# First k-tile of a mixer and FFN layer: half of its modulation summed on TensorE, larger first transfers, and rk's share of that k-tile moved there

## The chip, the cores and the metric

The kernel runs on one core of a Trainium2 chip. The metric is the device time of one execution in microseconds, the median of three runs. The engines are TensorE (PE; its weight loads are shown apart as PEld), VectorE (DVE), ScalarE (ACT), GpSimd (POOL) and SyncE (SP), which here only issues transfers.

## The reference

One layer over 256 tokens of width 1024, all in float32:

```
mod = silu(c) @ w_ada + b_ada            # six vectors of 1024: sh1, sc1, g1, sh2, sc2, g2
h = x * (1 + sc1) + sh1
y = token_mixer(h, ...)                  # h @ w_in -> mq mk mv rq rk rv rg g_a g_r, then
                                         # attention, retention, gates, two projections, w_out
x = layer_norm(ALPHA * x + g1 * y)
h = x * (1 + sc2) + sh2
y = conv_ffn(h, ...)                     # gate and up (2816 columns), conv of width 3, gelu, down
x = layer_norm(ALPHA * x + g2 * y)
```

w_in has 6656 columns: mq, mk, mv, rq and rk 512 each, then rv, rg, g_a and g_r of 1024. Nothing of h exists until the first two vectors of the modulation do, and these need silu(c) times 1024 x 2048 weights.

## The kernel before

**Precision.** Each float32 product is made of three fp32r products: a weight tile `raw` is split into `whi` (ScalarE copies it, rounding) and `wlo` (VectorE subtracts), the moving or stationary activations into `hh` and `hl`; hi x hi, hi x lo and lo x hi are summed in PSUM. A split of 1024 columns is one ScalarE and one VectorE instruction.

**Phase A (lines 160 to 352)** goes over h's eight k-tiles j of 128 rows. A k-tile's modulation is needed as a column on partitions, so VectorE multiplies the transposed weights of k-tile j (`m<j>`: 128 x 2048, the columns of 1 + sc1 and of sh1) by `srow`, silu(c) spread over all partitions, and sums each row (`ada`, L212; for j = 0 `ada0`, L220 to L228). Then h's k-tile is formed (`h1` parts 1 and 2: `hh`, L253 or L255, and `hl`, L258 and L260), and TensorE multiplies it with k-tile j of three column blocks: a (mq, mk), b (mv, rq) and g (half of g_a's k-tiles 0 to 3), each 1024 columns wide, 12 products of 128 x 512 per block (`x_prod`, L286). Eight PSUM banks `pa` are held through the phase: a and g share banks 0 to 3 (a0's result is copied out at once, L310, and added at the end of the phase, L964), b has banks 4 to 7.

**Transfers.** `UNITS` is the order written by hand in which raw tiles are loaded, four buffers of 1 MB (`RAW_BUFS`) in a ring; `load_A` issues the next one as soon as the program text has passed the last reader of the oldest, and the issue waits on SP's queue for that reader. `m0` is cut in four (`Q4`), its first piece on ScalarE's queue, everything else on SP's; a0 and b0 are one tile, cut in four.

**The start.** Until the modulation's vector c has landed, TensorE runs three matmuls on the identity (`WARM`, L185). Then `rows` (L192) spreads silu(c): eight transposes of a broadcast column (L197) into PSUM banks 6 and 7, `srow_p`. `ada0` has four reductions over 512 columns each, reading `srow_p` from PSUM: the first 512 rows of the weights for both vectors, then the last 512, whence the order of columns in `modT[0]` (L1333); `sums` adds them and the bias. `BUSY` stands for two float32 matmuls on m0's data (L207), whose result is not used. ScalarE copies `srow_p` to `srow` for the later k-tiles (L199).

**Phase B** streams the other weights as units of 1 MB (`weights`, `xstat`, `wstat8`), two halves of 1024 columns each; `prep_halves` splits them (L1206, L1220) up to `LOOKAHEAD` halves ahead. Its first two units are winB's columns of rk: h's eight k-tiles against 512 columns, two products sets (tokens 0 to 127 and 128 to 255) in two banks; at the end `rk_done` (L456) copies the banks into `S["rqk", t]` on ScalarE. Before the first of its products `evac_A` frees phase A's banks, and rope on mq and mk follows on VectorE (L942 to L946).

Of the kernel before, what the change touches and what calls it, by code (L numbers as in the profile page):

```python
# [30 lines left out]
Q4 = (0, 512, 1024, 1536, 2048)  # L31
HALVES = (0, 1024, 2048)
MERGED = 2
BUSY = 2
# [3 lines left out]
UNITS = ("m0", "a0b0", "g0", "m1", "b1g1", "m2", "b2g2", "m3", "b3g3", "a1a2", "m4", "a3", "a4b4", "m5", "a5b5",  # L38
# [18 lines left out]
def _body(nc, a, out, pe, act, dve, sp, cst, wts, big, tmp, ps, dram):  # L57
# [6 lines left out]

    place = {0: ("H", 0), 1: ("H", 1), "3a": ("Ya", 0), "6a": ("Ya", 1), "3b": ("Yb", 0), "6b": ("Yb", 1)}
# [94 lines left out]
    def load_A():  # L160

        if not units:
            return
        u = units.pop(0)
        j = int(u[-1])
        if u[0] != "m" and j and u[:2] != "a1" and u != "a3":
            load_x(j)
        cuts = Q4 if u in ("m0", "a0b0") else HALVES if j < 4 and u[0] in "mb" else (0, 2048)
        t = raw_tile()
        if u in ("g0", "a1a2", "a3"):  # L170
# [5 lines left out]
        for i in range(len(u) // 2):  # L176
            raws[u[2 * i:2 * i + 2]] = t[:, i * 1024:(i + 1) * 1024] if u[0] != "m" else t
# [14 lines left out]
    def rows(dst, cols):  # L192

        ps_ = [bank(6 + c) for c in range(2)]
        for c, p in enumerate(ps_):
            for i in range(4):
                pe.transpose(p[:, i * 128:(i + 1) * 128],  # L197
                             cols[:, c * 4 + i:c * 4 + i + 1].to_broadcast([128, 128]), ident)
        return ps_, lambda c: act.activation(dst[:, c * 512:(c + 1) * 512], ps_[c], AF.Copy)  # L199
# [3 lines left out]
    srow_p, srow_copy = rows(srow, sc)  # L203

    for i in range(BUSY):
        raw = raws["m0"]
        pe.matmul(bank(5), raw[:, i * 128:i * 128 + 128], raw[:, :512], start=True, stop=True)  # L207
# [7 lines left out]
    sums = cst.tile([128, 2, 3], F32, name="sums")  # L215
    dve.tensor_scalar(sums[:, :, 2], bcol[:, 0:2, 0], 0.0, None, op0=OP.add)

    def ada0(raw):

        junk = tmp.tile([128, 1024], mybir.dt.bfloat16, name="junk", bufs=1)  # L220
        for q in range(2):
            for i in range(2):
                w = raw[:, (2 * q + i) * 512:(2 * q + i + 1) * 512]
                dve.tensor_tensor_reduce(out=junk[:, :512], in0=srow_p[q], in1=w, scale=1.0, scalar=0.0,
                                         op0=OP.mult, op1=OP.add, accum_out=sums[:, i, q:q + 1])
            if q == 0:
                srow_copy(0)
        dve.tensor_reduce(mod[:, 0:2, 0], sums, mybir.AxisListType.X, OP.add)  # L228
# [35 lines left out]
    def halve(name, w=1024, between=None):  # L264

        raw = raws.pop(name)
        hi, lo = whl[name] = new_hl()
        for c in range(0, 1024, w):
            o = slice(c, c + w)
            act.activation(hi[:, o], raw[:, o], AF.Copy)  # L270
# [4 lines left out]
    def x_prod(name, ks, first=False, last=False, w=1024):  # L275


        j, b0, ws = int(name[1]), dict(a=0, b=4, g=0)[name[0]], whl[name]
        x = [hh, hh, hl]
        what = dict(zip((2, 1, 3), (((0, 0), (1, 1)), ((2, 0),), ((0, 0), (1, 1), (2, 0)))))[ks]  # L280
        turns = [(xi, k, c, t) for c0 in range(0, 1024, w) for xi, k in what for c in range(c0, c0 + w, 512)
                 for t in range(2)]
        if ks == 3:
            turns.sort(key=lambda e: e[2:])
        for xi, k, c, t in turns:
            pe.matmul(pa[b0 + c // 512 * 2 + t], x[xi][:, j, t * 128:(t + 1) * 128], ws[k][:, c:c + 512],  # L286
                      start=first and (xi, k) == (0, 0), stop=last and xi == 2)
# [7 lines left out]

    h1(0, 0)
    h1(0, 1)
    halve("a0", 512)
    srow_copy(1)
    h1(0, 2)  # L300
# [10 lines left out]
    g_prod(0, 2)  # L311
    g_prod(0, 1)
# [42 lines left out]
    main = []  # L355
    steps = []

    def weights(src, mm0, mm1):

        n = 2 * len(main)  # L360
        main.append(src)
        for i, mm in enumerate((mm0, mm1)):
            steps.append(((n + i,), (n + i,), lambda ts, mm=mm: mm(*ts[0])))
# [10 lines left out]
    def xstat(name, u0, xh, xl, nk, banks_of, done):  # L374
        for u in range(nk // 4):
            def mk(half, u=u):
                def mm(hi, lo):
                    bk = banks_of()
                    for t in range(2):
                        for kk in range(2):  # L380
                            k = u * 4 + half * 2 + kk
                            mm3(bk[t], xh(k)[:, t * 128:(t + 1) * 128], xl(k)[:, t * 128:(t + 1) * 128],
                                hi[:, kk * 512:(kk + 1) * 512], lo[:, kk * 512:(kk + 1) * 512],
                                k == 0, k == nk - 1)
                    if k == nk - 1:
                        done(bk)
                return mm
            weights(a[name][u0 + u], mk(0), mk(1))
# [62 lines left out]
    S = {}  # L451
    ghh, ghl = (lambda k: hh[:, k]), (lambda k: hl[:, k])

    def rk_done(bk):
        for t in range(2):
            act.activation(S["rqk", t][:, 512:1024], bk[t], AF.Copy)  # L456

    xstat("winB", 0, ghh, ghl, 8, lazy(two_banks), rk_done)
# [498 lines left out]
    def evac_A():  # L957
        v = slot(4, [128, 2, 512])
        for t in range(2):
            S["rqk", t] = slot(f"R{t}", [128, 1024])  # L960
        for t in range(2):
            for c in range(2):
                o = qk[t][:, c * 512:c * 512 + 512]
                dve.tensor_tensor(o, pa[2 * c + t], o, OP.add)  # L964
# [204 lines left out]
    for sec, at in ((2, (6, 7, 9, 10)), (3, (11, 12, 13, 14)), (4, (16, 18, 19, 20)), (5, (38, 41, 44, 47))):  # L1169
        for u in range(4):  # L1170
            done = (lambda sec=sec: rows_done(sec)) if sec > 3 else (lambda: None)
            extra.setdefault(at[u], []).append((a["ada2"][sec - 2, u], ada_unit(sec, u, done)))
    stream = []
    for i, src in enumerate(main):
        stream.append((src, None))
# [4 lines left out]
    def load_next():  # L1180
        if stream:
            src, fn = stream.pop(0)
            loaded.append((load_raw(src), fn))

    def prep_halves():
# [4 lines left out]
        def raw_halves():  # L1190
            while loaded:
                raw, fn = loaded.pop(0)
                for half in range(2):
                    if fn:
                        chain.append((raw, half, fn))
                    else:
                        yield raw[:, half * 1024:(half + 1) * 1024], half
# [3 lines left out]
        def first():  # L1201
            src, half = next(it, (None, None))
# [3 lines left out]
            act.activation(hi, src, AF.Copy)  # L1206
            return src, half, hi

        ahead = None
        while True:  # L1210
# [7 lines left out]
            src, half, hi = cur  # L1218
            lo = wts.tile([128, 1024], F32R, tag="wlo", name="wlo", bufs=HL_BUFS)
            dve.tensor_tensor(lo, src, f(hi), OP.subtract)  # L1220
# [152 lines left out]
```

## Time and profile before

| | |
|---|---|
| median of 3 runs | 427.49 us (427.38 to 427.71) |
| the profiled execution | 428.27 us |
| its span, first to last instruction | 426.5 us |
| TensorE busy | 416.9 us |
| VectorE busy | 368.1 us |
| ScalarE busy | 244.8 us |
| bytes read from HBM | 104.15 MB, 247 GB/s over the span |

Times in the views are in microseconds from the start of the span. In a timeline each line is: start, duration, engine, line of the code, operation, output <- inputs, shape, count, and in brackets the idle time of the engine before it with what ended it. Lines of the same kind are merged, so the duration of an "x4" runs from the first start to the last end. The chain of work that ended last is followed back from the last instruction and lists start, duration and what was running. Window lines give each engine's busy time, the granted clock, the DMA engines' busy share and GB/s. Transfer lines give the size and the time from issue to landing.

### The profile page before, as it was taken

To read this page: it belongs to the slowest core of one execution; us is meant where nothing else is said; L and a number is where in the kernel's file an instruction comes from. 1 tells how busy PE (TensorE), PEld (TensorE's weight loads), DVE (VectorE), ACT (ScalarE), POOL (GpSimd) and SP (SyncE) were. 2 spreads that over 40 slices of the span, in tenths; PEclk is the share of its full clock that TensorE was granted. 3 is DMA by queue.
4 is the path that set the end of the run, shared out by engine and by line. 5 is a ranking of instruction groups with operands and counts; after the bars stand their busy time and mean duration, and the time that the engine had idled before them with its cause. 6 is when DMAs were issued, how large, how long until landed. Compare 5 with 4: busy or idle time off the path is not lost.

```text
span 426.5 us, 5818 instructions
## 1 busy us (share of the span) xinstructions
PE 416.9 (98%) x2130; PEld 348.9 (82%) x2130; DVE 368.1 (86%) x608; ACT 244.8 (57%) x389; POOL 7.2 (2%) x18
## 2 busy tenths in 40 slices
PE   8999999999999999999999999999999999999992
PEld 4787888877878888888889899888888888888882
DVE  5888999979997999898778887999999888789576
ACT  4667558779764488534353885654545545455400
POOL 0000000100000000001000000100000000000000
PEclk9999999999999999999999999999999999999998
DMA  8999988869468868789552085985876776440001
GB/s 271 407 410 366 408 289 354 311 273 303 171 238 330 288 250 314 285 341 378 211 197 100 1 290 204 350 295 190 310 254 232 281 287 232 191 191 2 1 26 74
DMA packets 19694, 105.60 MB, mean 248 GB/s; under 512 B 2641, under 2 KB 4561, under 8 KB 8913
## 3 DMA queue, kind: packets, MB, share of 16 engines
q1 hardware_dynamic: 18144, 99.97, 62.5%
q0 software_dynamic: 1376, 4.99, 3.5%
q8 instruction: 17, 0.28, 0.3%
q10 hardware_dynamic: 144, 0.26, 0.2%
q14 instruction: 13, 0.10, 0.1%
HBM read 104.15 MB, written 1.06 MB: 247 GB/s over the span
## 4 chain that ended last, share of the span: by engine, by line
PE 96%; DMA 2%; DVE 1%; issue 0%; ACT 0%; POOL 0%; DVEq 0%; POOLq 0%
PE P L111 17%; PE P L113 17%; PE P L112 17%; PE P L120 15%; PE P L286 11%; PE P L122 8%; DMA raw<-in_strm 2%; PE P L665 1%; PE P L668 1%; PE P L667 1%; PE P L952 1%; PE P L1004 1%; PE P L1023 1%; PE P L1047 1%; PE P L207 1%; PE P L185 1%
## 5 line engine op out<-in xcount | busy, mean ns | idle before, releaser
L1220 DVE TENSOR_TENSOR wlo<-raw,whi 128x1024 fp32r<-128x1024 f32 x118 | 141.9, 1218 | 13.7 <-ACT whi L1206 13.6
L1206 ACT ACTIVATE whi<-raw 128x1024 fp32r<-128x1024 f32 x118 | 122.8, 1056 | 44.1 <-PE P L113 19.7
L111 PE MATMUL P<-whi,AH 128*128 128x512 f32 (+1 forms) x168 | 65.9, 392 | 0.0
L113 PE MATMUL P<-whi,AH 128*128 128x512 f32 (+1 forms) x168 | 64.0, 381 | 0.0
L112 PE MATMUL P<-wlo,AH 128*128 128x512 f32 (+1 forms) x168 | 63.8, 380 | 0.0
L212 DVE CUSTOM_DVE_ANT_0 junk<-raw,srow 128x1024 bf16<-128x1024 f32 x46 | 56.0, 1218 | 0.2
L286 PE MATMUL P<-whi,AH 128*128 128x512 f32 x160 | 42.5, 392 | 0.4 <-ACT AH L255 0.3
L120 PE MATMUL P<-AYa,whi 128*128 128x512 f32 x144 | 39.2, 394 | 0.0
L120 PE MATMUL P<-AYb,whi 128*128 128x512 f32 x144 | 38.6, 390 | 0.0
L111 PEld LDWEIGHTS P<-whi,AH 128*128 128x128 f32 x168 | 31.6, 188 | 6.7 <-issue 1.3
L113 PEld LDWEIGHTS P<-whi,AH 128*128 128x128 f32 x168 | 31.6, 188 | 6.2
L286 PEld LDWEIGHTS P<-whi,AH 128*128 128x128 f32 x160 | 29.8, 188 | 8.4 <-ACT AH L255 1.2
L112 PEld LDWEIGHTS P<-wlo,AH 128*128 128x128 f32 x168 | 31.7, 189 | 5.5
L436 ACT ACTIVATE A<-P 128x256 f32<-128x256 f32 x36 | 13.7, 381 | 34.1 <-PE P L122 32.2
L120 PEld LDWEIGHTS P<-AYb,whi 128*128 128x128 f32 x144 | 27.0, 188 | 6.0
L270 ACT ACTIVATE whi<-raw 128x1024 fp32r<-128x1024 f32 (+1 forms) x26 | 21.8, 857 | 16.8 <-DMA raw<-in_strm 15.0
L273 DVE TENSOR_TENSOR wlo<-raw,whi 128x1024 fp32r<-128x1024 f32 (+1 forms) x26 | 24.7, 977 | 5.8 <-ACT whi L270 5.5
L120 PEld LDWEIGHTS P<-AYa,whi 128*128 128x128 f32 x144 | 25.1, 190 | 3.6
L122 PEld LDWEIGHTS P<-AYa,wlo 128*128 128x128 f32 x144 | 22.0, 189 | 2.8
L286 PE MATMUL P<-wlo,AH 128*128 128x512 f32 x80 | 23.5, 391 | 0.1
L122 PE MATMUL P<-AYb,wlo 128*128 128x256 f32 x144 | 23.1, 283 | 0.0
L122 PE MATMUL P<-AYa,wlo 128*128 128x256 f32 x144 | 22.9, 282 | 0.0
(269 smaller groups left out, 712.3 us busy)
## 6 DMA issues: line engine op xcount, KB each, us to landing
raw<-in_ada SPq DMA_DIRECT2D x16, 1024.0 KB, 5.6
raw<-in_wup SPq DMA_DIRECT2D x11, 1024.0 KB, 5.8
raw<-in_wgate SPq DMA_DIRECT2D x11, 1024.0 KB, 5.7
raw<-in_wdown SPq DMA_DIRECT2D x11, 1024.0 KB, 4.9
raw<-in_winB SPq DMA_DIRECT2D x10, 1024.0 KB, 6.5
raw<-in_strm SPq DMA_DIRECT2D x8, 1024.0 KB, 7.0
raw<-in_strm SPq DMA_DIRECT2D x12, 512.0 KB, 7.6
raw<-in_winGr SPq DMA_DIRECT2D x4, 1024.0 KB, 6.2
```

The lines of the kernel that those rows point to most:

```text
L111: pe.matmul(o, lh, rh, start=start, stop=False)
L112: pe.matmul(o, lh, rl, start=False, stop=False)
L113: pe.matmul(o, ll, rh, start=False, stop=stop)
L120: pe.matmul(o, wh[:, k * 128:(k + 1) * 128], x2[k], start=k == 0, stop=False)
L122: pe.matmul(o[:, :256], wl[:, k * 128:(k + 1) * 128], x2[k][:, 0], start=False, stop=k == n - 1)
L212: dve.tensor_tensor_reduce(out=junk[:, rows], in0=raw[:, rows], in1=srow[:, rows], scale=1.0, scalar=0.0, op0=OP.mult, op1=OP.add, accum_o ...
L270: act.activation(hi[:, o], raw[:, o], AF.Copy)
L273: dve.tensor_tensor(lo[:, o], raw[:, o], f(hi[:, o]), OP.subtract)
L286: pe.matmul(pa[b0 + c // 512 * 2 + t], x[xi][:, j, t * 128:(t + 1) * 128], ws[k][:, c:c + 512], start=first and (xi, k) == (0, 0), stop=la ...
L436: act.activation(t, p[:, 256:], AF.Copy)
L1206: act.activation(hi, src, AF.Copy)
L1220: dve.tensor_tensor(lo, src, f(hi), OP.subtract)
```

## The change

- `m0` is one transfer of 1 MB on ScalarE's queue. a0 and b0's tile is cut in two instead of four. g0's tile becomes `r0g0`: k-tile 0 of rk's 512 columns, then g0.
- Only the first four transposes are made ahead of the sum (`spread(0)`). `ada0` sums the first 512 rows of the weights on VectorE (two reductions) and the last 512 on TensorE: eight float32 matmuls with a 128 x 128 block of weights as stationary operand and one column of silu(c) as moving operand, into two columns of bank 5. A matmul of 128 x 128 on m0's data follows, whose result is not used. VectorE adds the bias and then bank 5. `BUSY` and `sums` are gone.
- The other four transposes (`spread(1)`) come after a0's first four products; both copies to `srow` come after a0.
- `x_prod("r0", ...)` makes rk's six products of k-tile 0 in banks 0 and 1, after b0's; ScalarE copies them into `S["rqk", t]`, whose slots are opened earlier.
- Phase B's first unit leaves out k-tile 0: its transfer, its split and its six products. `rk_done` adds the banks on VectorE to what lies in `S["rqk", t]`.

The diff, without the parts that only pass the new column offset on:

```diff
-Q4 = (0, 512, 1024, 1536, 2048)
-BUSY = 2
-UNITS = ("m0", "a0b0", "g0", "m1", "b1g1", ...
+UNITS = ("m0", "a0b0", "r0g0", "m1", "b1g1", ...
...
-        cuts = Q4 if u in ("m0", "a0b0") else HALVES if j < 4 and u[0] in "mb" else (0, 2048)
+        cuts = HALVES if u == "a0b0" or j < 4 and u[0] in "mb" else (0, 2048)
...
-    def rows(dst, cols):
-        ps_ = [bank(6 + c) for c in range(2)]
-        for c, p in enumerate(ps_):
-            for i in range(4):
-                pe.transpose(p[:, i * 128:(i + 1) * 128],
-                             cols[:, c * 4 + i:c * 4 + i + 1].to_broadcast([128, 128]), ident)
-        return ps_, lambda c: act.activation(dst[:, c * 512:(c + 1) * 512], ps_[c], AF.Copy)
+    def spread(c):
+        p = bank(6 + c)
+        for i in range(4):
+            pe.transpose(p[:, i * 128:(i + 1) * 128],
+                         sc[:, c * 4 + i:c * 4 + i + 1].to_broadcast([128, 128]), ident)
+        return p
...
-    srow_p, srow_copy = rows(srow, sc)
-    for i in range(BUSY):
-        raw = raws["m0"]
-        pe.matmul(bank(5), raw[:, i * 128:i * 128 + 128], raw[:, :512], start=True, stop=True)
+    srow_p = [spread(0)]
...
     def ada0(raw):
         junk = tmp.tile([128, 1024], mybir.dt.bfloat16, name="junk", bufs=1)
-        for q in range(2):
-            for i in range(2):
-                w = raw[:, (2 * q + i) * 512:(2 * q + i + 1) * 512]
-                dve.tensor_tensor_reduce(out=junk[:, :512], in0=srow_p[q], in1=w, scale=1.0, scalar=0.0,
-                                         op0=OP.mult, op1=OP.add, accum_out=sums[:, i, q:q + 1])
-            if q == 0:
-                srow_copy(0)
-        dve.tensor_reduce(mod[:, 0:2, 0], sums, mybir.AxisListType.X, OP.add)
+        acc = bank(5)
+        for i in range(2):
+            for k in range(4):
+                w = raw[:, 1024 + (2 * k + i) * 128:1024 + (2 * k + i + 1) * 128]
+                pe.matmul(acc[:, i:i + 1], w, sc[:, 4 + k:5 + k], start=k == 0, stop=k == 3)
+        pe.matmul(bank(4)[:, :128], raw[:, :128], raw[:, :128], start=True, stop=True)
+        for i in range(2):
+            dve.tensor_tensor_reduce(out=junk[:, :512], in0=srow_p[0], in1=raw[:, i * 512:(i + 1) * 512], scale=1.0,
+                                     scalar=0.0, op0=OP.mult, op1=OP.add, accum_out=mod[:, i, 0:1])
+        m = mod[:, 0:2, 0]
+        dve.tensor_tensor(m, m, bcol[:, 0:2, 0], OP.add)
+        dve.tensor_tensor(m, acc[:, :2], m, OP.add)
...
     halve("a0", 512)
-    srow_copy(1)
     h1(0, 2)
+    a0 = whl["a0"]
+    for c in (0, 512):
+        for t in range(2):
+            pe.matmul(pa[c // 512 * 2 + t], hh[:, 0, t * 128:(t + 1) * 128], a0[0][:, c:c + 512], start=True, stop=False)
+    srow_p.append(spread(1))
+    for xi, k in ((hh, 1), (hl, 0)):
+        for c in (0, 512):
+            for t in range(2):
+                pe.matmul(pa[c // 512 * 2 + t], xi[:, 0, t * 128:(t + 1) * 128], a0[k][:, c:c + 512], start=False,
+                          stop=xi is hl)
+    srow_copy(0)
+    srow_copy(1)
     halve("b0", 512)
     load_A()
+    halve("r0")
     halve("g0")
     load_A()
-    x_prod("a0", 2, True, False, 512)
-    x_prod("a0", 1, False, True, 512)
-    x_prod("b0", 2, True, False, 512)
+    x_prod("b0", 2, True, False)
     x_prod("b0", 1)
     for i in range(4):
         act.activation(qk[i % 2][:, i // 2 * 512:i // 2 * 512 + 512], pa[i], AF.Copy)
-    g_prod(0, 2)
-    g_prod(0, 1)
+    x_prod("r0", 3, True, True, cs=(0,))
+    for t in range(2):
+        act.activation(S["rqk", t][:, 512:], pa[t], AF.Copy)
+    x_prod("g0", 3, True, cs=(512, 0))
...
     def rk_done(bk):
         for t in range(2):
-            act.activation(S["rqk", t][:, 512:1024], bk[t], AF.Copy)
+            o = S["rqk", t][:, 512:1024]
+            dve.tensor_tensor(o, bk[t], o, OP.add)
-    xstat("winB", 0, ghh, ghl, 8, lazy(two_banks), rk_done)
+    xstat("winB", 0, ghh, ghl, 8, lazy(two_banks), rk_done, 1)
```

More of the change, by code (lines that the diff above doesn't have):

```diff
@@ L175, in load_A @@
         load_cuts(t, src, cuts, (lambda: load_x(0)) if u == "a0b0" else None, act if u == "m0" else sp)
-        for i in range(len(u) // 2):
-            raws[u[2 * i:2 * i + 2]] = t[:, i * 1024:(i + 1) * 1024] if u[0] != "m" else t
+        c = 0
+        for n in (u[i:i + 2] for i in range(0, len(u), 2)):
+            w = dict(m=2048, r=512).get(n[0], 1024)
+            raws[n] = t[:, c:c + w]
+            c += w
     for i in range(RAW_BUFS):
@@ L267, in halve @@
         hi, lo = whl[name] = new_hl()
-        for c in range(0, 1024, w):
-            o = slice(c, c + w)
+        n = raw.shape[-1]
+        for c in range(0, n, min(w, n)):
+            o = slice(c, c + min(w, n))
             act.activation(hi[:, o], raw[:, o], AF.Copy)
@@ L273, in halve, with x_prod @@
             dve.tensor_tensor(lo[:, o], raw[:, o], f(hi[:, o]), OP.subtract)
-    def x_prod(name, ks, first=False, last=False, w=1024):
-        j, b0, ws = int(name[1]), dict(a=0, b=4, g=0)[name[0]], whl[name]
+    def x_prod(name, ks, first=False, last=False, w=1024, cs=(0, 512)):
+        j, b0, ws = int(name[1]), dict(a=0, b=4, g=0, r=0)[name[0]], whl[name]
         x = [hh, hh, hl]
         what = dict(zip((2, 1, 3), (((0, 0), (1, 1)), ((2, 0),), ((0, 0), (1, 1), (2, 0)))))[ks]
-        turns = [(xi, k, c, t) for c0 in range(0, 1024, w) for xi, k in what for c in range(c0, c0 + w, 512)
-                 for t in range(2)]
         if ks == 3:
-            turns.sort(key=lambda e: e[2:])
+            turns = [(xi, k, c, t) for c in cs for t in range(2) for xi, k in what]
+        else:
+            blocks = [cs] if w == 1024 else [(c,) for c in cs]
+            turns = [(xi, k, c, t) for b in blocks for xi, k in what for c in b for t in range(2)]
         for xi, k, c, t in turns:
@@ L293, in _body @@
     ga = slot(12, [128, 4, 512])
+    for t in range(2):
+        S["rqk", t] = slot(f"R{t}", [128, 1024])
     h1(0, 0)
@@ L310, in _body @@
         act.activation(qk[i % 2][:, i // 2 * 512:i // 2 * 512 + 512], pa[i], AF.Copy)
-    g_prod(0, 2)
-    g_prod(0, 1)
+    x_prod("r0", 3, True, True, cs=(0,))
+    for t in range(2):
+        act.activation(S["rqk", t][:, 512:], pa[t], AF.Copy)
+    x_prod("g0", 3, True, cs=(512, 0))
     WB = (512, 1024, 1024, 512)
@@ L387, in mk @@
                 return mm
[L388 removed]
+            weights(a[name][u0 + u], mk(0), mk(1), 512 * k0 if u == 0 else 0)
     bank_i = [0]
@@ L1191, in raw_halves @@
             while loaded:
-                raw, fn = loaded.pop(0)
+                raw, fn, c0 = loaded.pop(0)
                 for half in range(2):
@@ L1196, in raw_halves @@
                     else:
-                        yield raw[:, half * 1024:(half + 1) * 1024], half
+                        yield raw[:, half * 1024:(half + 1) * 1024], half, slice(0 if half else c0, 1024)
         it = raw_halves()
         def first():
-            src, half = next(it, (None, None))
+            src, half, o = next(it, (None,) * 3)
             if src is None:
```

46 lines of the change are left out of this document (25 added, 21 removed).

## The prediction

> **What bounds the kernel now.** I read the head of the page, the chain of work that ended last, the timeline of the first 18 us, and then the DMA and window views of the same stretch.
>
> ```profile
> span 426.5 us, 5818 instructions
> PE 416.9 (98%) x2130; PEld 348.9 (82%) x2130; DVE 368.1 (86%) x608; ACT 244.8 (57%) x389; POOL 7.2 (2%) x18
> PE 96%; DMA 2%; DVE 1%; issue 0%; ACT 0%; POOL 0%; DVEq 0%; POOLq 0%
> ```
>
> TensorE is busy for 98% of the span and carries 96% of the chain. So only two things can move the time: when TensorE gets its first real product, and how long it stands or runs slowly after that.
>
> ```profile
> 3.93 1.95 PE P L197 x8
> 5.87 1.72 PE P L207 x2
> 7.64 1.14 PE P L207 x2
> 8.79 7.46 DMA raw<-in_strm
> 17.25 0.59 ACT AH L255
> 17.89 16.79 PE P L286 x72
> 34.68 30.24 PE P L286 x132
> ```
>
> The chain has one interruption in 65 us: the transfer issued at 8.79 (b1g1's first half), then ScalarE's modulated x of the second k-tile (L255), then products without a break. 132 products in 30.24 us are 0.229 us each; that is the pace used below.
>
> ```profile
> 5.06 0.69 DVE L224 CUSTOM_DVE_ANT_0 junk<-P,raw 128x512 bf16<-128x512 f32 x1 [0.92 <-PE P L197]
> 7.36 0.69 DVE L224 CUSTOM_DVE_ANT_0 junk<-P,raw 128x512 bf16<-128x512 f32 x1
> 8.09 0.16 DVE L228 TENSOR_REDUCE mod<-sums 128x2 f32<-128x6 f32 x1
> 8.29 0.60 DVE L253 TENSOR_SCALAR AH<-AYa,mod 128x128 fp32r<-128x128 f32 x2
> 8.78 0.70 PE L286 MATMUL P<-whi,AH 128*128 128x512 f32 x2
> 9.54 0.73 PE L286 MATMUL P<-wlo,AH 128*128 128x512 f32 x2
> 16.28 1.06 ACT L270 ACTIVATE whi<-raw 128x1024 fp32r<-128x1024 f32 x1 [1.24 <-DMA raw<-in_strm]
> 17.89 1.20 PE L286 MATMUL P<-whi,AH 128*128 128x512 f32 x4 [0.34 <-ACT AH L255]
> ```
>
> Before the first product, VectorE decides: four reductions from 5.06 to 8.05, their sum at 8.09, x modulated at 8.29, first product 8.78. The start of the reductions is held by the transposes (L197), not by a transfer. From 8.78 to 17.89 stand 36 products (a0, b0, g0), 36 x 0.229 = 8.24, so 0.87 us of the 9.11 is lost: about 0.4 in a0, where the third product starts at 9.54 instead of 9.24, and about 0.5 ahead of 17.89.
>
> **The change, part by part.**
>
> *m0 as one transfer.* It is needed whole now, because TensorE's half lies behind VectorE's.
>
> ```profile
> 1.25 1.88 SPq L98 DMA_DIRECT2D raw<-in_strm  x4
> raw<-in_strm ACTq DMA_DIRECT2D x1, 256.0 KB, 2.9
> raw<-in_strm SPq DMA_DIRECT2D x1, 256.0 KB, 4.2
> 4.00:8.00 4.00, 3.94 (x11) 2.30 (x12) 2.88 (x9) 1.15 (x2) 0.00 (x0) 1.00 1.00 321
> 12.00:16.00 4.00, 4.00 (x19) 3.32 (x18) 2.94 (x5) 3.00 (x5) 0.00 (x0) 1.00 1.03 413
> ```
>
> The piece on ScalarE's queue landed 2.9 us after its issue at 0.80, at 3.7; m0's last piece, the third of the four SP issues (1.25 + 2 x 0.47 = 2.2), landed 4.2 later, at 6.4. With 2 KB rows the engines moved 321 GB/s (4 to 8 us), with longer rows 413 (12 to 16). The remaining 0.79 MB at 413 GB/s take 1.9 us: 5.6 if m0 has the engines to itself. It doesn't: a0b0's first half stands on SP's queue from 1.25. If that half's 0.52 MB all go between, 6.9. I take 6.1, near the old 6.4, with 5.6 and 6.9 as ends. The Trainium skill, "DMA: Bandwidth & Descriptors", section "Queues, rings and completion order", says that a DMA engine serves its queues in turn, packet by packet; by that m0 gives up a part of the bandwidth and 5.6 is not reached. The traces here can't show it for these two queues, as their large transfers don't overlap before the change.
>
> *The sum on TensorE.* Four reductions become two (2 x 0.77 = 1.5, done by 7.6 and so covered); TensorE gets eight matmuls of one column.
>
> ```profile
> 1.42 0.29 PEld L185 LDWEIGHTS P<-ident 128*128 128x128 f32 x1 [1.42 <-POOL ident L141]
> 1.42 0.50 PEld L185 LDWEIGHTS P<-ident 128*128 128x128 f32 x2 [1.42 <-POOL ident L141]
> 3.90 1.97 PE L197 MATMUL P<-ident,sc 128*128 128x128 f32 x8
> 75.64 1.03 PE L952 MATMUL P<-ident,A2a 128*128 128x128 f32 x8
> 5.67 1.06 PE L207 MATMUL P<-raw 128*128 128x512 f32 x1
> 8.17 0.59 PE L207 MATMUL P<-raw 128*128 128x512 f32 x1
> ```
>
> An f32 matmul is two passes, each with its weight load (L185: three matmuls, six loads), so 16 passes. A one-column pass is nowhere in this trace. Eight 128-column passes take 1.97 us early (0.25 each) and 1.03 at 75 us (0.13 each); a second load ended 0.21 after the first. Bounds: 16 x 0.13 = 2.1 and 16 x 0.25 = 3.9. I take 0.14 and a tail of 0.2, 2.5 us, near the lower end, because 127 of the 128 streamed columns fall away. The final add then stands where the reduce stood, and from there to the first product went 8.78 - 8.09 = 0.69. First product: 6.1 + 2.5 + 0.06 + 0.69 = 9.35, so 0.57 later than before. Ends: 5.6 + 2.1 + 0.75 = 8.45 and 6.9 + 3.9 + 0.75 = 11.55. While TensorE sums, nothing else in its queue could run: the filler matmul and a0's products stand behind.
>
> *BUSY's two matmuls go.* They lay inside the wait, so they cost nothing; but the rows of L207 show what they covered. The same shape takes 1.06 at 5.67 and 0.59 at 8.17, and the transposes above 0.25 and 0.13: TensorE ran at half rate until after 6.5 us and at full rate from about 7.64, although the windows print a granted clock of 1.00 there. Half rate ended after some 3.7 us of unbroken work (3.93 to 7.64 in the chain); the stretch before, with pauses, had not ended it. After the change TensorE has four transposes (to about 4.8), then nothing until m0 lands, then one-column passes. I charge 0.3 us for about 0.6 us of a0 at half rate; ends 0 and 1.85 (3.7 us of products at half rate lose half).
>
> *The other four transposes* move in behind a0's first four products: 4 x 0.13 = 0.52 at full rate, in a place where about 0.4 was lost anyway. *r0:* six products (6 x 0.229 = 1.37) go from the first winB half, where TensorE never stood, to the first k-tile. From the first product to the second k-tile's first: 42 x 0.229 + 0.52 = 10.14, so 19.49. Before, with the same six products added, it was 17.89 + 1.37 = 19.26. Net **+0.23**.
>
> *What must be ready at 19.49.*
>
> ```profile
> 13.01 0.58 ACT L310 ACTIVATE A2a<-P 128x512 f32<-128x512 f32 x1
> 23.44 0.76 PEld L286 LDWEIGHTS P<-whi,AH 128*128 128x128 f32 x4 [0.24 <-ACT AH L255]
> 28.94 0.30 PEld L286 LDWEIGHTS P<-whi,AH 128*128 128x128 f32 x2 [0.18 <-ACT AH L255]
> ```
>
> b1's transfer: its slot is m0's, free when the filler matmul ends (about 9.3; before, 8.79), and it queues behind transfers already issued, so the later issue costs nothing. The first 2.2 MB move at 413 instead of 321 GB/s (1.5 us sooner), r0's 0.26 MB cost 0.6: it lands about 0.9 earlier than 16.26. The tighter path is ScalarE's: two copies of r0's banks now stand ahead of b1's whi. r0's products end at 9.35 + 0.52 + 30 x 0.229 + 0.4 = 17.1; copies about 0.6 after the second bank, whi 1.06, x 0.58: 19.4, just under 19.49. Taken as 0; if it slips, 0.6. The two short waits at 23.44 and 28.94 (0.24 and 0.18, of which TensorE's stream shows about half) go, as TensorE now arrives later: **-0.2**. SP gets fewer issues (m0 1 for 4, a0b0 2 for 4), POOL none.
>
> *winB's end of it.*
>
> ```profile
> 62.43 1.28 DVE L964 TENSOR_TENSOR A2a<-P,A2a 128x512 f32<-128x512 f32 x2
> 68.55 2.35 DVE L1220 TENSOR_TENSOR wlo<-raw,whi 128x1024 fp32r<-128x1024 f32 x2
> 70.42 0.39 PE L112 MATMUL P<-wlo,AH 128*128 128x512 f32 x1
> 76.77 1.07 ACT L456 ACTIVATE AR<-P 128x512 f32<-128x512 f32 x2
> ```
>
> The third half's wlo ends about 69.75 and is used at 70.42: 0.67 of slack. VectorE's way there starts with a7's banks (62.43), and TensorE now has 1.37 us less to do between a7 and that half. VectorE took a7's banks without an idle gap (the row at 62.43 has no bracket), so it, not TensorE, was late there before, and a part is absorbed; taken as 0, ends 0 and 0.7. The first half's split is 512 columns shorter on both engines. rk's bank is added on VectorE (2 x 0.68) instead of copied on ScalarE (2 x 0.55), at a place where later halves are far ahead: 0.
>
> **Sum:** +0.23 - 0.2 + 0.3 = +0.33 us. The profiled execution took 428.27 (span 426.5 and 1.77 around it), 0.78 over the median; the difference is carried to the median: 427.49 + 0.33 = 427.8.
>
> **The rivals.**
> *Half rate stays (slower).* The pause from 4.8 to 6.1 and the one-column passes don't count as the work that ended half rate before, and a0 and b0 begin at half rate for another 3.7 us: +1.85 instead of +0.3, 429.4. For it: L185's stretch with pauses did not bring full rate. Against: the passes and the filler keep the queue busy for 3 us. It decides once more than 1.4 us of half-rate loss come together, given the other terms.
> The Trainium skill, "TensorE: Matmul & The Clock Gate", section "What's actually happening", says the clock starts at half and is released after a window of about 3.4 us of sustained work that runs free of the program; by that figure an unlucky window would cost 1.7, an estimate, and the time be about 429.2. The L207 rows agree with a halved start.
> *m0 early (faster).* m0 alone at 5.6 and TensorE's passes no longer than VectorE's 1.5: first product 5.6 + 1.6 + 0.75 = 7.95, 1.4 sooner than in the sum, no half-rate products: 427.49 + 0.33 - 0.3 - 1.4 = 426.1; with the passes at 0.13, 426.6. For it: larger rows move 413. Against: a0b0 shares the engines and the early passes ran 0.25.
> *The gap returns.* ScalarE's r0 copies delay b1's whi: the moved products then fill nothing, +0.6: 428.4.
>
> **How the numbers follow.** What this measurement can tell from no change is about 0.2%, 0.85 us: 426.6 to 428.3. The sum's case 0.31 (own range 427.0 to 428.4); half rate stays 0.31; m0 early 0.28; the gap returns 0.10, split between same and slower. So faster 0.28, same 0.36, slower 0.36. Range 426.2 to 429.9: the early case without its last tenth, and the half-rate case with half a microsecond of late summing.
>
> **What would show it.** In the timeline after: the one-column matmuls start between 5.6 and 6.9; the first L286-type product near 9.35; the product spacing there 0.23 (0.45 if half rate stays); no idle ahead of b1's first product near 19.5; winB's first half six products shorter and no wait on wlo near 70. It is wrong if the first product comes before 8.5 or after 10.2, or if the spacing stays at 0.45 for over 1.5 us.

## The result: 1.15% slower, and the profile after

| | median | range | ratio to before, 95% interval |
|---|---|---|---|
| before | 427.49 us | 427.29 to 427.71 | |
| after | 432.47 us | 432.04 to 432.78 | 1.0115 (1.0102 to 1.0128) |

Each row has five executions. The change costs 4.98 us; the prediction was 427.8 with a range of 426.2 to 429.9. The profiled execution of after took 432.78 us. The head of its page and its line of the chain's shares:

```profile
span 431.1 us, 5836 instructions
PE 420.3 (98%) x2144; PEld 353.3 (82%) x2144; DVE 367.6 (85%) x607; ACT 243.4 (56%) x390; POOL 7.2 (2%) x18
PE 88%; DVE 6%; DMA 3%; issue 1%; ACT 1%; DVEq 0%; SPq 0%; ACTq 0%
```

TensorE is still busy for 98%. Its 14 extra instructions are worth little, and yet it is busy for 3.4 us more: the same work got slower. Where, the chain that ended last shows in order of time (start, duration, what ran):

```profile
1.24 4.79 DMA raw<-in_strm
6.17 3.54 PE P L222 x16
9.71 0.64 PE P L223 x2
10.44 2.05 PE P L308 x4
12.48 0.85 PE P L198 x4
13.34 3.03 PE P L313 x8
16.36 23.15 PE P L289 x102
39.52 26.83 PE P L289 x117
```

m0's transfer, the sixteen one-column passes (L222), the filler, a0's products (L308, L313), then products without a break. In before this chain had VectorE's reductions covered by the filler and its first product at 8.78. TensorE's timeline of the same stretch (PEld's rows are left out):

```profile
4.68 1.11 PE L198 MATMUL P<-ident,sc 128*128 128x128 f32 x4 [0.76 <-DVE sc L192]
6.17 3.54 PE L222 MATMUL P<-sc,raw 128*128 128x1 f32 x16 [0.37 <-DMA raw<-in_strm]
9.57 0.78 PE L223 MATMUL P<-raw 128*128 128x128 f32 x2
10.44 2.05 PE L308 MATMUL P<-whi,AH 128*128 128x512 f32 x4
12.28 1.06 PE L198 MATMUL P<-ident,sc 128*128 128x128 f32 x4
12.99 2.06 PE L313 MATMUL P<-wlo,AH 128*128 128x512 f32 x4
14.84 1.52 PE L313 MATMUL P<-whi,AH 128*128 128x512 f32 x4
16.20 1.09 PE L289 MATMUL P<-whi,AH 128*128 128x512 f32 x4
```

The first product comes at 10.44, 1.66 later than in the profile of before. And four products of one shape take 2.05 at 10.44 and 2.06 at 12.99, but 1.09 at 16.20: TensorE is at half rate until nearly 16 us. The gap of 0.34 ahead of k-tile 2 is gone (TensorE's rows have no bracket from 6.17 to 24 us), and no wait stands at winB's third half; what was lost by then stayed lost. VectorE and ScalarE at the same place:

```profile
7.30 0.16 DVE L228 TENSOR_TENSOR mod<-mod,first 128x2 f32<-128x2 f32 x1
9.75 0.16 DVE L229 TENSOR_TENSOR mod<-P,mod 128x2 f32<-128x2 f32 x1 [2.28 <-PE P L222]
4.22 0.21 ACT L191 ACTIVATE sc<-first 128x8 f32<-128x8 f32 x1 [1.49 <-DMA first<-in_first]
```

VectorE's half of the sum is ready at 7.46 and waits 2.28 us for TensorE's. ScalarE gets the vector c at 4.22; in before it did at 3.44.

### The profile page after: what moved, and what is told of

It is laid out like the page before. It is cut to its first block, busy times and chain, and to the rows that moved or that the text cites. A ratio compares the mean times of both kernels' runs of the same rounds, so it can differ in the third digit from the quotient of the medians.

```text
span 431.1 us, 5836 instructions
## 1 busy us (share of the span) xinstructions
PE 420.3 (98%) x2144; PEld 353.3 (82%) x2144; DVE 367.6 (85%) x607; ACT 243.4 (56%) x390; POOL 7.2 (2%) x18
## 4 chain that ended last, share of the span: by engine, by line
PE 88%; DVE 6%; DMA 3%; issue 1%; ACT 1%; DVEq 0%; SPq 0%; ACTq 0%
PE P L119 15%; PE P L110 14%; PE P L112 14%; PE P L111 14%; PE P L289 12%; PE P L121 8%; DVE wlo L1240 3%; DMA raw<-in_winB 2%; DMA raw<-in_strm 1%; PE P L687 1%; PE P L690 1%; PE P L689 1%; PE P L222 1%; PE P L1043 1%; PE P L313 1%
## 5 line engine op out<-in xcount | busy, mean ns | idle before, releaser
L1240 DVE TENSOR_TENSOR wlo<-raw,whi 128x1024 fp32r<-128x1024 f32 (+1 forms) x118 | 141.4, 1213 | 13.6 <-ACT whi L1226 13.3
L1226 ACT ACTIVATE whi<-raw 128x1024 fp32r<-128x1024 f32 (+1 forms) x118 | 122.2, 1053 | 44.0 <-PE P L112 19.7
L110 PE MATMUL P<-whi,AH 128*128 128x512 f32 (+1 forms) x166 | 65.2, 393 | 0.0
L112 PE MATMUL P<-whi,AH 128*128 128x512 f32 (+1 forms) x166 | 63.2, 380 | 0.0
L289 PE MATMUL P<-whi,AH 128*128 128x512 f32 x156 | 41.3, 390 | 0.0
L110 PEld LDWEIGHTS P<-whi,AH 128*128 128x128 f32 x166 | 31.2, 188 | 6.6 <-issue 1.3
L112 PEld LDWEIGHTS P<-whi,AH 128*128 128x128 f32 x166 | 31.2, 188 | 6.2
L289 PEld LDWEIGHTS P<-whi,AH 128*128 128x128 f32 x156 | 29.3, 188 | 6.5 <-ACT A L348 0.4
L275 DVE TENSOR_TENSOR wlo<-raw,whi 128x1024 fp32r<-128x1024 f32 (+1 forms) x27 | 25.2, 966 | 7.8 <-ACT whi L272 7.6
L272 ACT ACTIVATE whi<-raw 128x1024 fp32r<-128x1024 f32 (+1 forms) x27 | 21.8, 844 | 12.5 <-DMA raw<-in_strm 12.5
```

The lines of the kernel that those rows point to most:

```text
L110: pe.matmul(o, lh, rh, start=start, stop=False)
L112: pe.matmul(o, ll, rh, start=False, stop=stop)
L1226: act.activation(hi[:, o], src[:, o], AF.Copy)
L1240: dve.tensor_tensor(lo[:, o], src[:, o], f(hi[:, o]), OP.subtract)
```

## The experiments

Theory: the loss is TensorE's rate. It runs at half rate until it has worked densely for a while, and one-column passes are not such work, while the matmuls of `BUSY`, which they replaced, were. Rival: the order of things at the start (m0 as one transfer, c late, the sum waiting) delays the first product, and the rest is the moved rk. Each ratio below is against executions of before that were taken together with the run; their medians are 427.51 to 427.75 us.

### One part at a time

**Before without BUSY.**

```diff
-BUSY = 2
+BUSY = 0
```

> The kernel before with BUSY = 0, nothing else changed. Half-rate theory: the first product stays near 8.7 us, since VectorE's four reductions set it, but TensorE stands from 5.9 to 8.7 and a0 and part of b0 then run at half rate (0.43 us between products instead of 0.23) for 3.5 to 5.5 us; 1.5 to 2.5 us slower, 429.0 to 430.0. Rival (the two BUSY matmuls are only filler, and full rate comes on its own or is not needed because a0 waits for wlo anyway): within 0.4 us of 427.5.

Measured 429.08 us, ratio 1.0037 (1.0023 to 1.005). TensorE's timeline:

```profile
8.82 1.19 PE L286 MATMUL P<-whi,AH 128*128 128x512 f32 x2 [2.91 <-DVE AH L253]
12.37 2.07 PE L286 MATMUL P<-whi,AH 128*128 128x512 f32 x6
14.28 0.62 PE L286 MATMUL P<-wlo,AH 128*128 128x512 f32 x2
```

The first product is where it was (8.82), yet 1.6 us are lost: two products take 1.19 here against 0.70 in before, and 0.62 only from 14.28. The two filler matmuls were no decoration: they brought the full rate before the first product.

**After with the start of before** (m0 and a0b0 in four, `rows`, four reductions, BUSY, a0's products in their old order; r0 and phase B as in after):

```diff
-    srow_p = [spread(0)]
+    srow_p, srow_copy = rows(srow, sc)
+    for i in range(BUSY):
+        pe.matmul(bank(5), raw[:, i * 128:i * 128 + 128], raw[:, :512], start=True, stop=True)
...
-                pe.matmul(acc[:, i:i + 1], w, sc[:, 4 + k:5 + k], start=k == 0, stop=k == 3)
+                dve.tensor_tensor_reduce(out=junk[:, :512], in0=srow_p[q], in1=w, ..., accum_out=sums[:, i, q:q + 1])
```

> The kernel after with the start of the kernel before: m0 and a0b0 in four pieces, all eight transposes first, four reductions on VectorE, BUSY. Left of the change: rk's six products of k-tile 0, their tile r0g0, the shorter first winB unit, the add on VectorE. If the loss is all in the start (half rate and late sum): 0.3 to 0.9 us faster than before, 426.6 to 427.2, since the six products fill the 0.5 us ahead of the second k-tile. If moving rk costs (ScalarE's copies ahead of b1, VectorE's add, wlo late for the third half): 0.5 to 1.5 us slower, 428.0 to 429.0.

427.72 us, 1.0012 (0.9997 to 1.0026): the same as before. Moving rk's columns neither costs nor brings what a measurement can tell; the expected gain of the closed gap did not come (see the repeated before below).

**Before with the sum on TensorE alone** (transfers of before, rk in phase B, no BUSY):

```diff
-    srow_p, srow_copy = rows(srow, sc)
+    srow_p = [spread(0)]
-    for i in range(BUSY):
...
+                pe.matmul(acc[:, i:i + 1], w, sc[:, 4 + k:5 + k], start=k == 0, stop=k == 3)
```

> The kernel before with the sum half on TensorE and the transposes split as in the change, BUSY gone, but m0 and a0b0 still in four pieces and rk not moved. Late-sum and half-rate theory together: c lands at 3.4 as before, m0's last piece at 6.4, sixteen passes of 0.22 us, first product near 10.7, half rate until 14 to 16 us; 3.5 to 5 us slower, 431 to 432.5. If the larger transfers are what makes the change slow: under 1 us slower, 427.5 to 428.5.

430.69 us, 1.0079 (1.0062 to 1.0095): the largest part, though less than the 431 to 432.5 that was expected. The first product stands at 9.98 instead of near 10.7, and half rate ends at about 12.6 instead of 14 to 16.

**Before with the larger transfers alone** (and four reductions on VectorE, BUSY, rk as in before):

```diff
-        cuts = Q4 if u in ("m0", "a0b0") else HALVES if j < 4 and u[0] in "mb" else (0, 2048)
+        cuts = HALVES if u == "a0b0" or j < 4 and u[0] in "mb" else (0, 2048)
```

> The kernel before with m0 as one transfer on ScalarE's queue and a0b0 in two, nothing else. c lands 0.8 us later, as in the changed kernel; the four reductions start when m0 is whole, near 6.1, and end near 9.1, first product near 9.8; BUSY's matmuls run from 6.1 to 9 and keep TensorE busy, so no product at half rate. If the start alone counts: about 1 us later, of which 0.5 is given back at the second k-tile: 427.9 to 428.6. If larger rows speed the first k-tiles up: 426.5 to 427.3.

428.33 us, 1.0021 (1.0012 to 1.003). c lands 0.57 later, and VectorE's reductions and the first product (9.34) move with it; the rate is full. Against their befores (427.51) the three parts give 3.18 + 0.82 + 0.21 = 4.21 of 4.98. They don't add up in full, and one difference is seen: half rate, which ends at about 12.6 with the sum alone, lasts to nearly 16 in after.

### What counts as work for the rate

**Passes 128 columns wide**, all else as in after:

```diff
-                pe.matmul(acc[:, i:i + 1], w, sc[:, 4 + k:5 + k], start=k == 0, stop=k == 3)
+                pe.matmul(acc[:, i * 128:(i + 1) * 128], w, sc[:, 4 + k:5 + k].to_broadcast([128, 128]),
+                          start=k == 0, stop=k == 3)
```

> After, with each of the sixteen weight passes 128 columns wide instead of one (the same weights, the silu column repeated 128 times; VectorE adds columns 0 and 128 of the sums). The arithmetic is the same. Theory (one-column passes do not count as work for the granted clock, 128-column passes do): a pass takes about as long as before at half rate (0.21 to 0.22 us against 0.22), the first product stays at 10.2 to 10.6, but the rate doubles earlier than the 15.76 of after, at 9.5 to 13, so that 1 to 2.5 us of the half-rate stretch go: 430.0 to 431.5. Rival A (the width does not matter, the rate is released a fixed time after products begin): product spacing 0.43 until about 15.8, 432.2 to 432.8. Rival B (a wide pass costs by its columns, 0.4 us): the passes end at 12.5, the first product at about 13, 433 to 435.

429.45 us, 1.0048 (1.0033 to 1.0063): **3.0 us of the 4.98 come back when each pass streams 128 times as many columns.** Its executions took 429.05 to 430.42 us, those of after 432.04 to 432.78. TensorE's timeline:

```profile
6.08 2.98 PE L222 MATMUL P<-sc,raw 128*128 128x128 f32 x16 [0.37 <-DMA raw<-in_strm]
9.79 1.15 PE L309 MATMUL P<-whi,AH 128*128 128x512 f32 x4 [0.51 <-DVE AH L255]
13.05 1.07 PE L290 MATMUL P<-whi,AH 128*128 128x512 f32 x4
```

The passes begin at the same place (6.08 against 6.17) and take no longer (2.98 against 3.54), and the first four products take 1.15, not 2.05. From first product to the first one of b0 are 3.26 us, in after 16.20 - 10.44 = 5.76: 2.5 us of half rate. The time that came back is more than the 1 to 2.5 us of the theory, as the rate doubled ahead of the first product.

**Passes 32 columns wide.**

```diff
+                pe.matmul(acc[:, i * 32:(i + 1) * 32], w, sc[:, 4 + k:5 + k].to_broadcast([128, 32]), ...
```

> After, with the passes 32 columns wide (1 column: 432.47; 128 columns: 429.45). Theory (what counts for the granted clock is the time in which columns stream, and 32 columns fill a quarter of what 128 do): the pass stays at 0.21 to 0.22 and the rate comes late, as with one column: 431.5 to 432.8. Rival (any pass wider than a column, or every instruction, counts): as with 128 columns, 429.0 to 430.5.

431.85 us, 1.0094 (1.008 to 1.0107). Sixteen passes took 3.59, and full rate came near 14.5: nearly as with one column. So it isn't the instruction that counts; passes of 128 columns count, and those of 32 hardly do. Whether 32 columns count more than one can't be read from this: one-column passes without the filler (below) have the full rate near 14.5 too.

**A TensorE kept at work**: wide passes, seven warm-up matmuls in alternating banks, one more behind the transposes.

```diff
-WARM = 3
+WARM, FILL = 7, 1
-        pe.matmul(bank(5)[:, :128], ident, ident, start=True, stop=True)
+        pe.matmul(bank(i % 4)[:, :128], ident, ident, start=True, stop=True)
     srow_p = [spread(0)]
+    for i in range(FILL):
+        pe.matmul(bank(i % 4)[:, :128], ident, ident, start=True, stop=True)
```

> After, with wide passes and TensorE kept at work from its first instruction: seven instead of three warm-up identity products, into alternating banks, and one more behind the transposes. Theory (the loss is half rate: TensorE stood too long in the first 9 us for the full clock): full rate from 5 to 9 us, wide passes at 0.11 to 0.2 each, first product at 8.3 to 9.6 and spacing 0.23 from there: 427.3 to 429.0. Rival A (the passes are bound by loading their weights, 0.22 whatever the clock): first product at 10.0 to 10.5, at full rate from there: 429.2 to 430.2. Rival B (the start does not matter, the loss is elsewhere): 432.0 to 432.8.

428.13 us, 1.0014 (1.0004 to 1.0023). Another 1.3 us: 4.34 of the 4.98 are gone.

```profile
5.94 2.07 PE L224 MATMUL P<-sc,raw 128*128 128x128 f32 x16
8.74 1.17 PE L311 MATMUL P<-whi,AH 128*128 128x512 f32 x4 [0.51 <-DVE AH L257]
74.95 1.03 PE L977 MATMUL P<-ident,A2a 128*128 128x128 f32 x8
```

A pass costs 0.13 at full rate. By 75 us the kernel is level with before: its rope transposes come at 74.95, in a second trace of before (below) at 75.05.

**The same with one-column passes** (the `pe.matmul(acc[:, i:i + 1], ...)` of after again).

> The run with seven warm-up products and one filler, but with the one-column passes of after: the fourth corner of narrow or wide passes, few or many warm-up products (after 432.47, wide 429.45, many and wide 428.13). Theory (one-column passes are no work for the granted clock, wide ones are): the warm-up products bring the full rate near 6 us, the passes themselves get shorter than 0.22, but during about 2 us of them TensorE counts as idle. If that is too little to take the rate away, 428.0 to 429.0, equal to many and wide within 0.9. If it takes the rate away, product spacing is 0.43 for some of the first products and the time 429.5 to 431.5. Rival (a one-column pass takes 0.22 at any rate, because its weight load bounds it): passes end 1.3 to 1.6 later than with wide passes and the time is 429.4 to 430.0 at full rate.

429.85 us, 1.0058 (1.0041 to 1.0075). This is the clearest of the runs. Its timeline, and then its windows (stretch and length, busy time of PE, PEld, DVE, ACT, POOL, granted clock, DMA share, GB/s):

```profile
5.85 2.35 PE L224 MATMUL P<-sc,raw 128*128 128x1 f32 x16
8.93 1.16 PE L310 MATMUL P<-whi,AH 128*128 128x512 f32 x4 [0.40 <-DVE AH L256]
10.43 2.06 PE L315 MATMUL P<-wlo,AH 128*128 128x512 f32 x4
13.79 1.09 PE L291 MATMUL P<-whi,AH 128*128 128x512 f32 x4
```
```profile
8.00:10.00 2.00, 1.60 (x9) 1.25 (x10) 1.73 (x5) 1.39 (x3) 0.00 (x0) 1.00 1.01 421
10.00:12.00 2.00, 2.00 (x9) 1.71 (x8) 0.62 (x3) 1.19 (x3) 0.00 (x0) 0.53 1.02 419
12.00:14.00 2.00, 2.00 (x7) 1.56 (x6) 1.91 (x4) 2.00 (x4) 0.00 (x0) 0.61 1.03 410
```

The full rate was there: four products in 1.16 at 8.93. Then, with TensorE busy without a pause, the granted clock falls to 0.53 and 0.61 as a mean of these stretches (0.50 from 10.2 to 13.4), and four products take 2.06, until 13.8. The fall comes at about 10.1, some 1.9 us after the last pass. So after a run of one-column passes the rate is taken away again; with wide ones it isn't, though TensorE stands longer there (0.51 ahead of 8.74, here 0.40 ahead of 8.93). (In the stretch ahead of the first change of clock these windows print 1.00 whatever the rate, so there the spacing of products must be read.) The Trainium skill, "TensorE: Matmul & The Clock Gate", section "What's actually happening", has the clock follow how busy TensorE was in the last window of about 3.4 us, and not a count of instructions. This trace agrees as far as it goes: the half rate lasts 3.4 us, from 10.1 to 13.5. It adds that a busy row of the profile is not yet that busyness.

### What bounds the start when the rate is full

**m0 on SP's queue**, all else as in after:

```diff
-        load_cuts(t, src, cuts, ..., act if u == "m0" else sp)
+        load_cuts(t, src, cuts, ..., sp)
```

> After, with m0 issued on SyncE's queue ahead of a0b0 instead of on ScalarE's. Theory (c's small transfer lands 0.78 late because it shares the DMA engines with m0 from two queues): c and x run beside m0 either way, but m0 now starts earlier than a0b0 and alone in its queue. If c lands again at about 3.4 and m0 at 5.3 to 5.9, the passes begin 0.3 to 0.9 earlier and the end comes 0.3 to 0.9 earlier: 431.5 to 432.2. Rival A (c is late from m0's bytes whichever queue carries them): c at 4.2, m0 at 6.1, no change, 432.3 to 432.8. Rival B (a0b0 behind m0 in one queue lands later): first half of a0b0 beyond 9.5, first product later than 10.5 and 432.8 to 433.5.

432.35 us, 1.0112 (1.0097 to 1.0127): no change. That is rival A's time, but not its mechanism: ScalarE had c at 2.54, earlier than in before (transposes at 3.71), while m0 held the passes until 6.43. So in after c's late landing was not on the path. **The same on the kept-busy kernel** (six warm-up matmuls, two fillers):

> The same as the run with wide passes and a kept-busy TensorE (six warm-up products, two behind the transposes), with m0 on SyncE's queue. Theory: m0's landing is then the bound of the passes; with m0 0.3 to 0.9 earlier the first product is at 7.7 to 9.2 and the end 0.3 to 0.9 earlier than that run: 426.6 to 428.5. Rival A (m0 lands no earlier on that queue): equal to that run within 0.3. Rival B (the first half of a0b0, queued behind m0, ends the wait ahead of the first product): the first product stands at a0b0's landing near 9.5, 428.0 to 429.2.

428.54 us, 1.0019 (1.0009 to 1.0029): passes at 6.37, first product 9.51, no better. The time is rival B's, the cause isn't: the wait ahead of the first product is for the passes, which end at 8.78, while a0's weights were there by 7.65.

**m0 in two halves on ScalarE's queue, TensorE's first**, on the kept-busy kernel without its filler (`for c0 in (1024, 0): act.dma_start(t[:, c0:c0 + 1024], ...)`).

> The run with many warm-up products and wide passes, without the filler behind the transposes, and with m0 in two transfers on ScalarE's queue, the half that TensorE sums first. Theory (with the rate regained, the start is bound by m0's last landing near 5.9 and the sixteen passes behind it): the passes begin at 5.0 to 5.6 and end by 7.6, VectorE's two reductions follow the second half at 6.0 to 6.3 and end at 7.5 to 7.8, the first product is at 8.1 to 8.6 instead of 8.74, and the time 427.3 to 428.0. Rival A (4 KB rows in two transfers land later: both halves near 6.4): first product at 8.8 to 9.3, 428.1 to 428.7. Rival B (TensorE stands between transposes and passes and loses the rate): spacing 0.43, 429 to 431.

429.59 us, 1.0045 (1.0033 to 1.0058): worse. VectorE's half landed last, and late; then TensorE's first products:

```profile
7.35 0.69 DVE L232 CUSTOM_DVE_ANT_0 junk<-P,raw 128x512 bf16<-128x512 f32 x1 [3.45 <-DMA raw<-in_strm]
9.77 1.19 PE L315 MATMUL P<-whi,AH 128*128 128x512 f32 x4 [1.70 <-DVE AH L261]
```

This shows one thing more about the rate. TensorE stood for 1.70 us ahead of its first product and still had the full rate there (1.19 for four) and behind it. A pause of 1.63 in the next run did not take it away either.

**m0 in quarters in their order of use**, on before with the sum alone, wide passes, five warm-up matmuls, a0b0 in two:

```diff
-        load_cuts(t, src, cuts, ..., act if u == "m0" else sp)
+        if u == "m0":
+            for c0 in (1024, 1536, 0, 512):
+                (act if c0 == 1024 else sp).dma_start(t[:, c0:c0 + 512], src[:, c0:c0 + 512])
```

> Before with the sum on TensorE and split transposes, passes 128 columns wide, five warm-up products in alternating banks, and m0 in four transfers in the order in which they are used: TensorE's two quarters first, VectorE's two last; a0b0 in two. rk stays in winB. Theory (the sum on TensorE itself costs nothing once it counts as work; what is left is when the last piece lands and what follows it): TensorE's passes run at 4.9 to 7.2, VectorE's last reduction begins when the last quarter lands at 6.3 to 6.6 and ends by 7.4, the first product is at 8.0 to 8.4 instead of 8.65 to 8.78 of before, at full rate: 426.7 to 427.3. Rival A (the sum on TensorE costs something beyond the rate, or a0's weights are late): first product no earlier than 8.6, 427.4 to 428.2. Rival B (full rate is lost): spacing 0.43, 428.5 or more.

428.38 us, 1.002 (1.0011 to 1.0029). The sum is early, and it brings nothing. VectorE, then ScalarE:

```profile
7.69 0.16 DVE L232 TENSOR_TENSOR mod<-P,mod 128x2 f32<-128x2 f32 x1
8.34 0.60 DVE L257 TENSOR_SCALAR AH<-AYa,mod 128x128 fp32r<-128x128 f32 x2 [0.49 <-DMA AYa<-in_strm]
7.92 1.15 ACT L274 ACTIVATE whi<-raw 128x512 fp32r<-128x512 f32 x2 [4.30 <-DMA raw<-in_strm]
```

x and a0's weights are the last to arrive now, and the first product stands at 8.83. **The same with a0b0 in four**, so that x stands behind 256 KB of a0:

```diff
-        cuts = Q4 if u == "m0" else HALVES if u == "a0b0" or j < 4 and u[0] in "mb" else (0, 2048)
+        cuts = Q4 if u in ("m0", "a0b0") else HALVES if j < 4 and u[0] in "mb" else (0, 2048)
```

> The run with m0 in quarters, TensorE's first, but a0b0 in four transfers as in before, so that x is queued behind 256 KB of a0 instead of 512 KB. In that run the sums were ready at 7.85, and the first product stood at 8.83 behind x (landed at about 8.3) and the high part of a0 (from 7.92). Theory (with the sum at full rate the start is bound by the landing of x and a0, not by the sum): x lands by 7.7, a0's first quarter at 7.0 to 7.3, VectorE's scaling starts at 7.9 right behind the sums, the first product is at 8.2 to 8.5, a0's second quarter follows at 8.1 to 8.5: 427.1 to 427.9. Rival A (the transfers are no earlier, since the queue only carries the same bytes in other pieces): first product at 8.7 to 8.9, 427.9 to 428.6. Rival B (TensorE then stands between a0's first and second quarter): first product at 8.3, but a pause of 0.3 to 0.6 behind two products, 427.5 to 428.2.

427.90 us, 1.0007 (0.9998 to 1.0016): the same as before. The first product came at 8.68, not at 8.2 to 8.5. VectorE:

```profile
6.25 0.69 DVE L228 CUSTOM_DVE_ANT_0 junk<-P,raw 128x512 bf16<-128x512 f32 x1 [2.35 <-DMA raw<-in_strm]
7.99 0.16 DVE L232 TENSOR_TENSOR mod<-P,mod 128x2 f32<-128x2 f32 x1
```

So the sum on TensorE, at full rate and with m0 and a0b0 in four transfers as in before, costs nothing; it also gains nothing, because m0's last quarter (6.25) and two reductions behind it set the sum at 7.99, where before had it at 8.09. No version tried beats before.

### What belongs to one execution

**Before with five warm-up matmuls in alternating banks**, a second trace of nearly the same kernel:

```diff
-WARM = 3
+WARM = 5
-        pe.matmul(bank(5)[:, :128], ident, ident, start=True, stop=True)
+        pe.matmul(bank(i % 4)[:, :128], ident, ident, start=True, stop=True)
```

> Before, with five warm-up products in alternating banks instead of three in one bank; they end at about the time of the three (3.9). Theory (before has its full rate from 7.46, ahead of its first product at 8.78, which VectorE's four reductions set): no change, 427.3 to 427.9, first product at 8.5 to 8.8. Rival (before too loses time to half rate in its transposes): the transposes, and with them the reductions and the first product, 0.2 to 0.5 earlier, 427.0 to 427.3. The same run shows whether the pause of 0.34 ahead of the second half-k-tile in the profile of before, and its 0.78 over its median, come back in another execution.

427.52 us, 0.9998 (0.9989 to 1.0008). Before lost nothing to the rate. TensorE's timeline:

```profile
8.65 0.70 PE L286 MATMUL P<-whi,AH 128*128 128x512 f32 x2 [0.43 <-DVE AH L253]
16.36 2.13 PE L286 MATMUL P<-whi,AH 128*128 128x512 f32 x8
75.05 1.03 PE L952 MATMUL P<-ident,A2a 128*128 128x128 f32 x8
177.96 0.60 PE L1142 MATMUL P<-ident,A8b 128*128 128x128 f32 x4
```

The gap of 0.34 ahead of k-tile 2 (inside the row at 16.36) is not there, the rope transposes at 75 us come 0.59 earlier than in the profile of before (75.64), and the span is 425.9 instead of 426.5. That gap was no fixed part of before. It hangs on b1g1's transfer, whose buffer is m0's, so that it is issued when the second `BUSY` matmul has read m0: at 8.79 in the profile of before, at 8.26 here, at 8.01 with rk moved alone, which has the start of before. The execution of before that was profiled, 0.78 above the median, had these matmuls late.

**After without its filler matmul.**

```diff
-        pe.matmul(bank(4)[:, :128], raw[:, :128], raw[:, :128], start=True, stop=True)
```

> After without the filler product behind the passes (two instructions of 0.2 at half rate that nothing reads). Theory of the rate: those 0.4 us of wide work less between passes and products; the first product stands where it did (it waits for VectorE) or 0.1 earlier, the rate comes no earlier: 432.0 to 433.0. Rival (the filler keeps a window full that would otherwise fail, or takes 0.2 from the first product): 431.5 to 431.9 or 433 to 435. By the drift: if the 0.7 us that after lost between 75 and 180 us in its profiled execution belongs to the kernel, this run loses 0.5 to 0.8 there too; if it belonged to that execution, 0 to 0.2.

431.65 us, 1.0093 (1.008 to 1.0106): 0.8 below after, more than expected; the full rate came at 14.5 instead of near 16, which the theory did not foresee. From the first product to the full rate it is 2.6 us with the sum alone, 4.2 here and 5.3 in after, all with one-column passes; what decides that is not shown. After, and then this run, at the two places of the last fence:

```profile
79.15 1.03 PE L974 MATMUL P<-ident,A2a 128*128 128x128 f32 x8
182.75 0.60 PE L1162 MATMUL P<-ident,A8b 128*128 128x128 f32 x4
```
```profile
78.48 1.03 PE L973 MATMUL P<-ident,A2a 128*128 128x128 f32 x8
181.52 0.60 PE L1161 MATMUL P<-ident,A8b 128*128 128x128 f32 x4
```

Against the repeated before, after is 4.10 late at the first place and 4.79 at the second, this run 3.43 and 3.56. The 0.69 that after lost in between are not a fixed part of the change; what they are stays open.

The end of the chain, at VectorE's last step before the program's end, in the repeated before, in the kept-busy run and in after:

```profile
422.70 0.40 DVEq L1369
```
```profile
422.71 0.40 DVEq L1393
```
```profile
427.49 0.40 DVEq L1390
```

The first two are equal, but the spans are 425.9 and 426.3. From this step to the end pass 3.2 us in before and its repeat, 3.6 in after and the kept-busy run: 0.4 us of the loss lie behind the last output's issue. With the larger transfers alone it is 3.4, with rk moved alone 3.4 too, with the sum alone 3.2; why was not found.

## Why the prediction was wrong, step by step

The prediction named signs of being wrong, and two of them are there: the first product comes after 10.2, and the spacing stays near 0.45 for more than 1.5 us.

**m0 whole at 6.1:** right, as a choice between its two ends; the passes begin at 6.17. **From the final add to the first product 0.69:** right, 9.75 to 10.44. **No idle at k-tile 2, no wait in winB:** right, and not only because TensorE came late: with rk moved alone neither is there.

**"I take 0.14 and a tail of 0.2, 2.5 us" failed.** The passes took 3.54, 0.22 each. The step argued that 127 of 128 streamed columns fall away. But at half rate one, 32 and 128 columns all cost about the same (3.54, 3.59, 2.98 with a part at full rate); the price falls to 0.13 and 0.15 with the rate (2.07 wide, 2.35 narrow). The working had the early price beside it, 0.25, as the other end, and this place is early. That is 1.04 of the 1.09 us by which the first product missed its 9.35.

**"I charge 0.3 us for about 0.6 us of a0 at half rate; ends 0 and 1.85" failed, and is the largest miss:** 2.5 us. The step saw that half rate ends after dense work and that the change takes BUSY away; it then charged only 0.6 us, with the passes and the filler in mind, which "keep the queue busy for 3 us". That isn't the work that counts. Its upper end failed too, as it counted one stretch of 3.7 us from the first product; half rate lasted from 10.44 to nearly 16. The rival "half rate stays" named the mechanism and the place, and the note that the passes may not count; its 429.4 lacked the passes' price and the longer stretch.

**"The difference is carried to the median" failed by about 0.5.** The gain of the closed gap (within +0.23) was read from an execution 0.78 above its median; a second trace has no such gap to close. The short waits (-0.2) are there in the second trace too (0.22 and 0.19 on the weight loads at 22.84 and 28.34). With rk moved alone they are gone, and yet from the first product to the rope transposes it is 66.38 us against 66.40: closing them brought nothing that shows. The moved rk alone measured +0.2, within what can't be told from no change.

**Not on the list:** 0.4 us at the program's end.

The sum, from the repeated before: first product 10.44 - 8.65 = 1.79, half rate 2.50, regained by 75 us 0.19, end 0.4: 4.5. The two spans differ by 5.2 (431.1 - 425.9); the other 0.7 is what after lost between 75 and 180 us, which stays open. The medians differ by 4.98.

## What to carry to other kernels

Before replacing filler work on TensorE by useful work, ask whether the new work streams as much: a run of narrow matmuls shows as busy in the profile and still leaves, or puts, TensorE at half rate. Read the rate from the duration of one shape at several places, and price an early matmul by an early row. Where a term of the sum is a wait seen once, look for it in a second execution before counting its removal as a gain.

## What the runs showed of the hardware

- One-column float32 passes with a 128 x 128 weight load took 0.22 us each at half rate, as much as passes of 32 columns, and 0.15 when most of them ran at full rate.
- The granted clock fell to half some 1.9 us after a run of them (2.35 us), though TensorE's rows show no pause longer than 0.40 there. With passes of 128 columns, pauses of 1.63 and 1.70 us did not bring it down.
- A transfer of 28 KB (c) reached ScalarE at 3.8 to 4.2 in the seven runs in which the other queue had m0 as one transfer of 1 MB with 8 KB rows, at 3.3 to 3.5 where that queue had 256 KB with 2 KB rows, and at 2.5 where it had none. The Trainium skill, "DMA: Bandwidth & Descriptors", section "Queues, rings and completion order", has an engine take its queues in turn, a packet at a time; that agrees with c being later beside the other queue. That the length of the rows decides is not shown: with two transfers of 512 KB and 4 KB rows c came at 3.40. In after it cost nothing, as m0 came later still; with the larger transfers alone it moved the first product by 0.56.
